# One encoder layer on one core: the last plain up-projection tiles become Strassen steps

## The chip, the core and the metric

The kernel runs on one core of a Trainium2 chip. The core has a matmul engine (TensorE, PE in the profile, with its weight loads as PEld), three engines for element-wise work (VectorE or DVE, ScalarE or ACT, GpSimd or POOL), a queue engine that starts transfers (SyncE or SP), 16 DMA engines that all queues share, an on-chip memory of 128 partitions (SBUF) and eight accumulation banks behind TensorE (PSUM). The engines run side by side and wait for each other by semaphores; each of ACT, DVE and POOL works through its own instructions strictly in order.

The metric is the device time of one execution in microseconds (us). Before the change the median of three runs is 526.61 us (526.12 to 527.57).

## The reference, cut to what matters

The layer is an RMSNorm, a combined input projection, a recurrent head group and an attention head group, an output projection, a residual sum, and an MLP. The change lies in the first half of the MLP:

```python
x = x + mix @ w_out[l]                                   # x: 512 rows of 1024
h = rms_norm(x, mlp_norm_g[l])
x = x + jnp.square(jax.nn.relu(h @ w_up[l])) @ w_down[l]   # w_up: 1024 x 4096
```

All of it is float32. The kernel leaves the normalising factor of `h` to the end (relu and square let it through as its square), so the up-projection multiplies the transposed rows of `x`, scaled by the gain, and the result is scaled per row when it is added to `x`.

## The kernel before, in words

**Precision.** TensorE takes a reduced float32 form, so each operand is split in two: a high part (a copy that rounds) and a low part (what the copy lost). `mm3` (L311) makes one product from three matmuls: high by high, high by low, low by high. Each weight chunk of 128 x 1024 is loaded to a raw tile, its high part `whi` is copied by ACT (`conv_hi`, L240) and its low part `wlo` is subtracted by DVE (`conv_lo`, L261). `feed` (L299) asks for both three chunks ahead of the chunk that TensorE multiplies.

**The MLP's halves.** The 4096 columns of `w_up` are done in two halves of 16 tiles of 128 columns. A half has an up-projection, whose results are relu'd, squared and kept on chip, and then a down-projection with `w_down`. The names that matter: `pu` are the PSUM tiles of the up-projection, `pd` those of the down-projection.

**Plain tiles and Strassen steps.** A plain tile (`up_tile`, L1558) multiplies one 128-column tile by all 512 rows: 8 blocks of the inner dimension, each three matmuls of 512 columns, 24 in all. Four such tiles can also be done as one group by one level of Strassen's scheme: inner dimension, columns and rows are cut in two, and seven products of sums take the place of eight. Each of the seven steps (`up_step`, L1574) has 24 matmuls of 256 columns. The kinds are named by their operands: `11`, `21` and `22` take a block of the weights as it is, `t1` to `t4` take sums of weight blocks (t1 = 12 + 11, t2 = t1 + 22, t3 = 12 + 22, t4 = t2 + 21). On the side of the rows, `11`, `21` and `t4` take unsummed quadrants, and `t1`, `t2`, `t3` and `22` take sums (`h_sums`, L1331), which DVE builds and which are then split into `hh` and `hl` (`split_h`, L1597). The sums are also written to DRAM (`hsd`) and read back for the second half.

**The results of a group.** The seven products collect in three PSUM banks (a, b, c). `quad_evac` (L1372) copies a bank aside on ACT after `11`, `t1` and `t2`, adds a copy and a bank on DVE after `22`, `t3` and `21`, and takes a relu on ACT after `t4`; the squares follow on ACT two steps later where `ON_ACT` (L58) says so, else on DVE. When two groups that belong together are done, DVE makes the sums for the down-projection (`up_pair`, L1285) and `next_a` begins to split them.

**The weight sums.** A raw tile `tw` takes block 12 by an ordinary load from SP, and blocks are added by transfers that accumulate, which only POOL's queue can start (`load_t`, L1177). t2 is made by such a transfer onto t1's tile once t1 is split (L277); t4 and t3 are made by DVE (L286, L281).

**Which group is what, and in which order.** `STEPS` (L54) is written out by hand for each half: before, the first half has four plain tiles (`n0` to `n3`) and three groups (4, 8, 12), the second half four groups (0, 8, 12, 4). Three plain tiles run side by side at the head of the first half (L1522 to L1531), the rows 4 to 7 of the transposed operand being turned by TensorE after their first block; the operand sums are made beside them. What is done beside a step is hung on it by hand in `late` (L1614): operand splits, the row squares `x1_sq` (L1267), loads. ACT, DVE, POOL and PE work in the order of the program; SP does not: its transfers are sent as soon as their buffers are free, in an order that a scheduler sets at build time.

**Ahead of the MLP.** The second half of the output projection is itself done by seven Strassen steps (`OSEQ`, L62); beside its last steps (`BES`, L1243) the first rows of the operand are turned (`h2_t`, L1207, and their low parts, `h2_l`, L1219) and the first weights are split.

**Buffers.** Raw weights: three stream tiles `wraw` and four `tw`. Split weights: four `whi` and four `wlo`. The four tiles `ts` that the down-projection will need share one large buffer with the residual rows `x1`, which are last read when the output projection ends. PSUM: four banks `pj`, two `gs`, two `et`.

Of the kernel before, what the change touches and what calls it, by code (L numbers as in the profile page):

```python
# [44 lines left out]
for _n, _w in (("w0", 4), ("w1", 4), ("w2", 4), ("w3", 4), ("cb", 4),  # L45
# [19 lines left out]
def up_steps(h):  # L65
    return [("n", int(s[1:])) if s[0] == "n" else (s.split(":")[1], int(s.split(":")[0])) for s in STEPS[h].split()]
# [32 lines left out]
def hybrid_kernel(ctx: ExitStack, tc, xw0, xw, xn, w_in, w_v, w_out, w_up, w_dn, gates, vecs, bias, fg, out):  # L99
# [90 lines left out]
    cu, cq, cd_ = {}, {}, []  # L190
    for h in range(2):
        for kind, f0 in up_steps(h):
            if kind == "n":
                cu[h, f0] = len(chunks)
                chunks.append(w_up[h * HF + f0])
            else:
                cq[h, f0, kind] = len(chunks)
                chunks.append((h, kind, f0, "u"))
# [37 lines left out]
    for (h, f0, kind), i in cq.items():  # L236
        if kind == "11" and (h, f0) != (0, 4):
            swap[i], swap[i + 1] = i + 1, i
# [22 lines left out]
    def conv_lo(i):  # L261
        if i < len(chunks):
# [11 lines left out]
            if isinstance(c, tuple) and len(c) == 4:  # L274
# [4 lines left out]
                elif kind == "22":  # L279
                    t = raws[cq[h, f0, "t3"]]  # L280
                    nc.vector.tensor_tensor(t, t, r, op=OP.add)  # L281
                elif kind in ("t2", "21"):
# [894 lines left out]
    def load_t(half, n, f0):  # L1177
        t = work.tile([P, 1024], FT, name="tw", tag="tw", bufs=4)
        nc.sync.dma_start(t, ublock(half, "12", f0))
        for b in {"t1": ("11",), "t2": ("11", "22"), "t3": ()}[n]:  # L1180
            nc.gpsimd.dma_start(t, ublock(half, b, f0), accum_op=OP.add)
        raws[cq[half, f0, n]] = t

# [65 lines left out]
    BES["s1"].update({1: lambda: (o_lo("22", 0), o_lo("22", 1), h2_t(0, "pj")), 2: lambda: h2_t(1, "pj"), 3: lambda: (conv_lo(C_WA + 8), h2_l(0))})  # L1249
    BES["22"].update({1: lambda: (h2_t(2, "pj"), h2_l(1)), 2: lambda: (h2_t(3, "pj"), conv_lo(C_WA + 9)), 3: lambda: (h2_l(2), h2_l(3))})  # L1250
    for w in OSEQ:
# [7 lines left out]
        if w in ("s3", "s4", "21"):  # L1259
            load_t(0, {"s3": "t1", "s4": "t2", "21": "t3"}[w], 4)  # L1260
# [20 lines left out]

    def h2k(k):
        return (h2h[:, k, :], h2l[k])
# [29 lines left out]
    def up_evac(ff, p):  # L1313
        q, c = ff // 2, slice((ff % 2) * TH, (ff % 2 + 1) * TH)
        for t in range(2):
            if (q, t) not in rb:
                rb[q, t] = g_("a")
            act(rb[q, t][:, c], p[:, t * TH:(t + 1) * TH], AF.Relu)
        if ff % 2:
            for t in range(2):  # L1320
                nc.vector.tensor_tensor(rb[q, t], rb[q, t], rb[q, t], op=OP.mult)
                rb_done.add((q, t))
            up_pair(q)


# [5 lines left out]
    def h_sums(k):  # L1331
        m, c = k // 2, slice((k % 2) * TH, (k % 2 + 1) * TH)
        if k % 2 == 0:
            for n in SUMS:
                hsum[n, m] = g_("hsum")
        a, b = hm.pop(k), hm.pop(k + 4)
        e, s2, s3, s4 = [hsum[n, m][:, c] for n in SUMS]
        nc.vector.tensor_tensor(e, b[:, right], a[:, right], op=OP.subtract)
        stt(s2, a[:, left], -1.0, e, op0=OP.mult, op1=OP.subtract)
        nc.vector.tensor_tensor(s3, a[:, left], a[:, right], op=OP.subtract)  # L1340
        stt(s4, b[:, left], -1.0, s2, op0=OP.mult, op1=OP.subtract)
# [156 lines left out]
    def load_s1(half, ts, qs=range(NQ)):  # L1498
        for q in qs:
            t = ts[:, q, :]  # L1500
            nc.sync.dma_start(t, wblock(half, "11", q))
            nc.gpsimd.dma_start(t, wblock(half, "12", q), accum_op=OP.add)
            raws[cd_[half] + 2 * q + 1] = t
# [9 lines left out]
    for half in range(2):  # L1513
        c0, cd = cu.get((half, 0)), cd_[half]
# [4 lines left out]
        start = 0  # L1519
        if half == 0:  # L1520
            start = 3
            pu = [ps_("pu", "pj") for _ in range(start)]  # L1522
            for k in range(KD):
                if k == 1:
                    for j in range(4, 8):
                        h2_t(j, "gs" if j < 6 else "et")
                        h2_l(j)
                for i in range(start):
                    mm3(pu[i], wk(c0 + i, k), h2k(k), k == 0, k == KD - 1)
                    if i == 0:  # L1530
                        feed(c0, k)  # L1531
                if k in (2, 3, 4, 5):
                    h_sums(k - 2)
                if k == 6:
                    x1_sq(0, 0)
                if k in (5, 7):
                    h_hi("t1", k // 7)
# [269 lines left out]
```

## Time and profile before

| | |
|---|---|
| median of three runs | 526.61 us (526.12 to 527.57) |
| the profiled execution | 526.41 us, its span 524.6 us |
| mean granted TensorE clock | 0.998 |
| busy in the span: PE, DVE, ACT, POOL | 517.3, 430.8, 350.1, 63.9 us |
| first up-projection | 201.1 to 285.2 us of the span |
| second up-projection | 361.4 to 442.0 us |

A row of the timeline holds the start and the duration of an instruction in us, its engine, its line, what it writes and reads by the program's names, and its shape. Matmuls overlap, so what one costs is the distance from its start to the next one's. A row of a line's answer has the number of instructions and their shortest, median and longest duration in ns. A row of the transfers ends with the size of each and the median time from its issue to its landing, in us. A row of windows has the stretch, its length, then the busy time and the count of PE, PEld, DVE, ACT and POOL, the clock, the share of the DMA engines and GB/s.

### The profile page before, as it was taken

The numbers are of one execution on the slowest core, as the hardware profiler recorded it, in microseconds if no ns is written. First come the engines' busy times: TensorE is split into PE (matmuls) and PEld (weight loads), VectorE is DVE, ScalarE is ACT, GpSimd is POOL, SyncE is SP. The second block draws the span as 40 slices with busy tenths as digits, with TensorE's granted clock in tenths as the row PEclk, the third lists the DMA queues.
The fourth block names the chain that finished last, engine by engine and source line by source line (L and its number), as shares of the span: only waits on it lengthen the run. The fifth ranks groups of instructions, "written<-read, shape, count | busy, mean of one in ns | idle before, by whom it ended". The sixth has DMA issues, their size and how long they took to land.

```text
span 524.6 us, 8196 instructions
## 1 busy us (share of the span) xinstructions
PE 517.3 (99%) x3021; PEld 442.9 (84%) x3021; DVE 430.8 (82%) x669; ACT 350.1 (67%) x566; POOL 63.9 (12%) x88
## 2 busy tenths in 40 slices
PE   9999999999999999999999999999999999999995
PEld 7857888777787688899999888889999999888884
DVE  6998985788887998898789987789656978986985
ACT  6579946668865748585578666565476677655664
POOL 0183000000000221001300312001101300131000
PEclk9999999999999999999999999999999999999999
DMA  7736545367696299848595899976978497799704
GB/s 287 226 89 198 161 150 180 102 171 212 186 295 207 62 188 277 323 130 196 131 229 135 222 272 280 305 269 161 300 221 202 113 229 214 157 286 264 183 1 161
DMA packets 39961, 104.62 MB, mean 199 GB/s; under 512 B 4944, under 2 KB 13264, under 8 KB 39920
## 3 DMA queue, kind: packets, MB, share of 16 engines
q1 hardware_dynamic: 32368, 78.10, 44.5%
q0 software_dynamic: 7408, 25.79, 26.7%
q8 instruction: 24, 0.39, 0.3%
q10 hardware_dynamic: 144, 0.20, 0.1%
q14 instruction: 17, 0.14, 0.1%
HBM read 95.59 MB, written 4.29 MB: 190 GB/s over the span
## 4 chain that ended last, share of the span: by engine, by line
PE 96%; DVE 2%; DMA 1%; SPq 0%; issue 0%; ACT 0%; DVEq 0%; ACTq 0%
PE pu L312 10%; PE pu L314 10%; PE pu L313 10%; PE pd L314 10%; PE pd L312 10%; PE pd L313 10%; PE pqk L312 3%; PE pqk L314 3%; PE pqk L313 3%; PE pwo L312 2%; PE pav L942 2%; PE pwo L314 2%; PE pwo L313 2%; PE pt L842 2%; PE ps L806 2%; PE pp L312 1%
## 5 line engine op out<-in xcount | busy, mean ns | idle before, releaser
L269 DVE TENSOR_TENSOR wlo<-wraw,whi 128x1024 fp32r<-128x1024 f32 x71 | 86.6, 1220 | 23.8 <-ACT whi L247 23.6
L247 ACT ACTIVATE whi<-wraw 128x1024 fp32r<-128x1024 f32 x67 | 70.7, 1056 | 32.4 <-PE pd L314 17.9
L313 PE MATMUL pd<-wlo,ah 128*128 128x512 f32 (+1 forms) x195 | 75.2, 386 | 0.0
L312 PE MATMUL pd<-whi,ah 128*128 128x512 f32 (+1 forms) x195 | 75.2, 386 | 0.0
L314 PE MATMUL pd<-whi,al 128*128 128x512 f32 (+1 forms) x195 | 75.2, 386 | 0.0
L247 ACT ACTIVATE whi<-tw 128x1024 fp32r<-128x1024 f32 x38 | 40.2, 1060 | 39.3 <-DMA tw<-in_w_up_dram 11.5
L313 PE MATMUL pu<-hl,whi 128*128 128x256 f32 x224 | 63.4, 283 | 0.0
L314 PE MATMUL pu<-hh,wlo 128*128 128x256 f32 x224 | 63.4, 283 | 0.0
L312 PE MATMUL pu<-hh,whi 128*128 128x256 f32 x224 | 63.4, 283 | 0.0
L269 DVE TENSOR_TENSOR wlo<-tw,whi 128x1024 fp32r<-128x1024 f32 x38 | 46.4, 1221 | 17.7 <-ACT whi L247 17.7
L312 PE MATMUL pu<-h2h,whi 128*128 128x256 f32 (+1 forms) x200 | 60.1, 300 | 0.0
L313 PE MATMUL pu<-h2l,whi 128*128 128x256 f32 (+1 forms) x200 | 60.0, 300 | 0.0
L314 PE MATMUL pu<-h2h,wlo 128*128 128x256 f32 (+1 forms) x200 | 60.0, 300 | 0.0
L312 PEld LDWEIGHTS pu<-hh,whi 128*128 128x128 f32 x224 | 43.0, 192 | 0.0
L313 PEld LDWEIGHTS pu<-hl,whi 128*128 128x128 f32 x224 | 43.0, 192 | 0.0
L314 PEld LDWEIGHTS pu<-hh,wlo 128*128 128x128 f32 x224 | 43.0, 192 | 0.0
L313 PEld LDWEIGHTS pd<-wlo,ah 128*128 128x128 f32 x195 | 36.6, 188 | 7.4
L314 PEld LDWEIGHTS pd<-whi,al 128*128 128x128 f32 x195 | 36.6, 188 | 7.3
L312 PEld LDWEIGHTS pd<-whi,ah 128*128 128x128 f32 x195 | 36.6, 188 | 7.3
L247 ACT ACTIVATE whi<-ts 128x1024 fp32r<-128x1024 f32 x24 | 25.4, 1060 | 25.7 <-PE pd L314 16.4
L313 PEld LDWEIGHTS pu<-h2l,whi 128*128 128x128 f32 x200 | 38.3, 191 | 1.3
L312 PEld LDWEIGHTS pu<-h2h,whi 128*128 128x128 f32 x200 | 38.3, 191 | 1.3
(275 smaller groups left out, 1214.8 us busy)
## 6 DMA issues: line engine op xcount, KB each, us to landing
wraw<-in_w_up_dram SPq DMA_DIRECT2D x25, 512.0 KB, 4.0
ts<-in_w_dn_dram POOLq DMA_DIRECT2D x24, 512.0 KB, 13.2
wraw<-in_w_dn_dram SPq DMA_DIRECT2D x24, 512.0 KB, 8.8
tw<-in_w_up_dram SPq DMA_DIRECT2D x15, 512.0 KB, 9.0
tw<-in_w_up_dram POOLq DMA_DIRECT2D x15, 512.0 KB, 8.0
wraw<-in_w_in_dram SPq DMA_DIRECT2D x13, 512.0 KB, 4.2
ts<-in_w_dn_dram SPq DMA_DIRECT2D x8, 512.0 KB, 6.5
tw<-in_w_dn_dram SPq DMA_DIRECT2D x8, 512.0 KB, 7.2
```

The source lines that it names most:

```text
L247: act(hi, raws[i], AF.Copy)
L269: nc.vector.tensor_tensor(lo, r, f(splits[i][0]), op=OP.subtract)
L312: nc.tensor.matmul(o, lhsT=a[0], rhs=b[0], start=bool(first), stop=False, skip_group_check=on)
L313: nc.tensor.matmul(o, lhsT=a[0], rhs=b[1], start=False, stop=False, skip_group_check=on)
L314: nc.tensor.matmul(o, lhsT=a[1], rhs=b[0], start=False, stop=bool(last), skip_group_check=on)
L806: nc.tensor.matmul(psq[p, u][e][:, :NK], lhsT=qs_[p, a][r, P * qt:P * qt + P], rhs=kks[p][r, b, w:w + NK], start=i == 0, stop=i == 2)
L842: nc.tensor.transpose(pt[:, i * P:(i + 1) * P], en[h][qt][:, k:k + P], ident)
L942: nc.tensor.matmul(pav[p][a, co], lhsT=vs[:, jt, h * DH:(h + 1) * DH], rhs=et[h, jt][:, ci], start=jt == 0 and i == 0, stop=jt == 3 and i ...
```

## The change

All 28 steps of the first half become Strassen steps, in a new order that begins with products of unsummed operands. In parts:

- `STEPS`, `QUADS`: the plain tiles go, group 0 comes; the first half is 0:11 8:11 4:11 0:21 8:21 0:t1 4:21 8:t1 and so on.
- Operand sums (`h_sum`): made one kind at a time, t1 and t2 on DVE, t3 and 22 on POOL, hung on the first steps. POOL has twelve instructions of 128 x 256.
- Weight sums of the first half: t4 of all four groups by an accumulating transfer (`RAW`), t3 of groups 0 and 8 too (`ADDED`); DVE keeps the t3 of 4 and 12.
- Squares of group 4 move from DVE to ACT, like those of the others (`ON_ACT`).
- The first step does its products with the operand's low parts last in each half (`head`).
- The rows 4 to 7 are turned inside the first two steps (`turn`); before, in one go after the first block. In the output projection's last steps the turns come one place earlier, and the low parts of two weight chunks move into the first step.
- The evacuations of the 21 blocks of groups 0, 8 and 4 are put off (`later`, `put`).
- Four of the eight row squares and the signs `nr2` move into the down-projection.
- The plain loads of `ts` and the accumulating transfers onto them are issued apart (`load_s1`, `add_s1`).

The diff, cut to its core:

```diff
-    "n0 n1 n2 4:11 4:t1 n3 4:t2 4:21 4:22 4:t3 8:11 8:t1 4:t4 8:t2 8:21 8:22 8:t3 12:11 12:t1 8:t4 12:t2 12:22 12:t3 12:21 12:t4",
+    "0:11 8:11 4:11 0:21 8:21 0:t1 4:21 8:t1 0:t2 0:22 0:t3 8:t2 4:t1 8:22 0:t4 8:t3 4:t2 8:t4 4:22 4:t3 12:11 12:t1 4:t4 12:t2 12:22 12:t3 12:21 12:t4",
...
-QUADS = ((4, 8, 12), (0, 8, 12, 4))
-ON_ACT = {(h, f, k) for h in range(2) for f in QUADS[h] if (h, f) != (0, 4) for k in ("21", "22", "t3", "t4")}
+QUADS = ((0, 8, 4, 12), (0, 8, 12, 4))
+AJ = {(0, 4), (1, 0)}
+ADDED = {(0, 0), (0, 8)}
+RAW = {(0, 0), (0, 4), (0, 8), (0, 12)}
+ON_ACT = {(h, f, k) for h in range(2) for f in QUADS[h] for k in ("21", "22", "t3", "t4")}
...
-                elif kind == "22":
+                elif kind == "22" and (h, f0) not in ADDED:
                     t = raws[cq[h, f0, "t3"]]
                     nc.vector.tensor_tensor(t, t, r, op=OP.add)
+                elif (h, f0) in RAW and kind == "t2":
+                    nc.gpsimd.dma_start(r, ublock(h, "21", f0), accum_op=OP.add)
+                    raws[cq[h, f0, "t4"]] = r
+                elif (h, f0) in RAW and kind == "21":
+                    emit_dma()
...
-    BES["s1"].update({1: lambda: (o_lo("22", 0), o_lo("22", 1), h2_t(0, "pj")), 2: lambda: h2_t(1, "pj"), 3: lambda: (conv_lo(C_WA + 8), h2_l(0))})
-    BES["22"].update({1: lambda: (h2_t(2, "pj"), h2_l(1)), 2: lambda: (h2_t(3, "pj"), conv_lo(C_WA + 9)), 3: lambda: (h2_l(2), h2_l(3))})
+    BES["s1"].update({1: lambda: (o_lo("22", 0), o_lo("22", 1), h2_t(0, "pj")), 2: lambda: h2_t(1, "pj"), 3: lambda: (h2_t(2, "pj"), h2_l(0))})
+    BES["22"].update({0: lambda: h2_l(1), 1: lambda: (h2_t(3, "pj"), h2_l(2)), 2: lambda: (h2_l(3), conv_hi(C_WA + 9)), 3: lambda: None})
...
-        if w in ("s3", "s4", "21"):
-            load_t(0, {"s3": "t1", "s4": "t2", "21": "t3"}[w], 4)
+        if w in ("s3", "s4", "21", "s1"):
+            load_t(0, *{"s3": ("t3", 0), "s4": ("t1", 0), "21": ("t1", 8), "s1": ("t1", 4)}[w])
...
+        if n == "t1":
+            nc.vector.tensor_tensor(o, b[:, right], a[:, right], op=OP.subtract)
+        elif n == "t2":
+            stt(o, a[:, left], -1.0, hsr["t1", m][:, c], op0=OP.mult, op1=OP.subtract)
+        elif n == "t3":
+            nc.gpsimd.tensor_tensor(o, a[:, left], a[:, right], op=OP.subtract)
+        else:
+            nc.gpsimd.tensor_tensor(o, a[:, left], b[:, left], op=OP.subtract)
+            nc.gpsimd.tensor_tensor(o, o, hsr["t1", m][:, c], op=OP.add)
         if k % 2:
-            for i, n in enumerate(SUMS):
-                nc.sync.dma_start(hsd[i][:, m * S:(m + 1) * S], hsum[n, m])
+            nc.sync.dma_start(hsd[SUMS.index(n)][:, m * S:(m + 1) * S], hsr[n, m])
...
+            head = half == 0 and (kind, f0) == ("11", 0)
...
+                if head:
+                    nc.tensor.matmul(o, lhsT=w[0], rhs=x[0], start=first, stop=False, skip_group_check=True)
+                    nc.tensor.matmul(o, lhsT=w[1], rhs=x[0], start=False, stop=False, skip_group_check=True)
+                    for k in range(4) if n % 4 == 3 else ():
+                        sl = slice((4 * e + k) * P, (4 * e + k + 1) * P)
+                        nc.tensor.matmul(o, lhsT=hi[:, sl], rhs=h_part(kind, k)[1], start=False, stop=n == 7 and k == 3, skip_group_check=True)
+                else:
+                    mm3(o, w, x, first, n == 7, True)
...
-                if n == 6:
+                if n == 6 and (half, kind, f0) != (0, "t2", 12):
                     next_a()
-            quad_evac(kind, f0, bank, keep, (half, f0, kind) in ON_ACT)
+            if half == 0 and kind == "21" and f0 < 12:
+                later.append(lambda: quad_evac("21", f0, bank, keep, True))
+            else:
+                quad_evac(kind, f0, bank, keep, (half, f0, kind) in ON_ACT)
...
+            late.update({(0, "11", 0): lambda: conv_lo(C_WA + 8), (0, "11", 3): lambda: conv_lo(C_WA + 9), (0, "11", 6): turn((4, 5)), (8, "11", 1): turn((6, 7)),
+                         (0, "11", 1): sums(*[("t3", k) for k in range(4)]), (8, "11", 0): sums(("t1", 0), ("t1", 1)), (8, "11", 5): split_h("t1", 0),
+                         (4, "11", 0): sums(("t1", 2), ("t1", 3), ("22", 0), ("22", 1), ("22", 2), ("22", 3)),
+                         (4, "11", 1): split_h("t1", 1), (0, "21", 0): sums(("t2", 0), ("t2", 1)),
+                         (0, "21", 5): split_h("t2", 0), (8, "21", 0): sums(("t2", 2), ("t2", 3)), (8, "21", 5): split_h("t2", 1),
+                         (0, "t1", 5): split_h("22", 0), (4, "21", 5): split_h("22", 1),
+                         (0, "t3", 3): put, (8, "t2", 3): put, (0, "t4", 3): put, (8, "t1", 1): split_h("t3", 0), (0, "t2", 1): split_h("t3", 1),
+                         (8, "t1", 5): lambda: load_t(0, "t3", 8, False), (0, "22", 1): lambda: add_t(0, "t3", 8),
+                         (8, "t2", 5): lambda: load_t(0, "t3", 4), (0, "t4", 5): lambda: load_t(0, "t1", 12, False), (4, "t2", 2): lambda: add_t(0, "t1", 12),
+                         (4, "t3", 5): lambda: load_t(0, "t3", 12),
+                         (0, "22", 7): xt(0, 0), (8, "t2", 7): xt(0, 1), (8, "22", 7): xt(1, 0), (4, "t2", 5): xt(1, 1), (4, "22", 5): room,
...
+            if half == 0 and j < 4:
+                x1_sq(2 + j // 2, j % 2)
```

More of the change, by code (lines that the diff above doesn't have):

```diff
@@ L236, in hybrid_kernel @@
     for (h, f0, kind), i in cq.items():
-        if kind == "11" and (h, f0) != (0, 4):
+        if kind == "11" and h:
             swap[i], swap[i + 1] = i + 1, i
@@ L1513, in hybrid_kernel @@
     for half in range(2):
-        c0, cd = cu.get((half, 0)), cd_[half]
+        cd = cd_[half]
         rb_done.clear()
@@ L1518, in hybrid_kernel, with room @@
         todo = deque((w, q) for _, w, q in seq)
[L1519 to L1537, printed above, removed]
[L1538 to L1546 removed]
+        def room():
             nonlocal ts
             ts = big.tile([P, NQ, 1024], FT, name="ts", tag="bigA")
[L1549 to L1551 removed]
         def next_a():
@@ L1615, in hybrid_kernel @@
         qs = QUADS[half]
-        for f0, f1 in zip(qs, qs[1:]):
+        for f0, f1 in zip(qs, qs[1:]) if half else ():
             late[f0, "t2", 0] = lambda f1=f1: load_t(half, "t1", f1)
@@ L1626, in hybrid_kernel @@
         if half == 0:
-            late[8, "t3", 4], late[12, "11", 4], late[12, "t2", 1], late[12, "t2", 7] = [load_1(q) for q in range(4)]
+            late[4, "t3", 4], late[12, "11", 4], late[12, "t2", 1], late[12, "t2", 7] = [load_1(q) for q in range(4)]
         else:
             late[12, "t3", 4], late[4, "11", 4], late[4, "t2", 1], late[4, "t2", 7] = [load_1(q) for q in range(4)]
-        for kind, f0 in up_steps(half)[start:]:
+        for kind, f0 in up_steps(half):
             ready = set(opdone)
             st["step"] = st.get("step", 0) + 1
-            if kind == "n":
-                up_tile(f0, late)
-            else:
-                up_step(kind, f0, late)
+            up_step(kind, f0, late)
         while pend_sq:
@@ L1700, in hybrid_kernel @@
                 load_s3(half, q)
+            if half == 0 and j < 4:
+                x1_sq(2 + j // 2, j % 2)
+                nr2[j] = consts.tile([P, 1], FT, name="nr2_%d" % j)
+            if half == 0 and j == 4:
+                for tt in range(4):
+                    nc.vector.tensor_scalar(nr2[tt], r2[tt], -1.0, None, op0=OP.mult)
             if half == 0 and j == 16:
```

114 lines of the change are left out of this document (40 added, 74 removed).

## The prediction

> **What bounds the kernel now.** I read the page first, then what TensorE waits for, then the stages by windows, then single rows of the timeline.
>
> ```profile
> span 524.6 us, 8196 instructions
> PE 517.3 (99%) x3021; PEld 442.9 (84%) x3021; DVE 430.8 (82%) x669; ACT 350.1 (67%) x566; POOL 63.9 (12%) x88
> ...
> PE 96%; DVE 2%; DMA 1%; SPq 0%; issue 0%; ACT 0%; DVEq 0%; ACTq 0%
> ```
> ```profile
> PE pwarm L142 <- PEq L1796: 0.8, 1, 0.8
> PE pxr L453 <- ACT h_hi L353: 0.2, 1, 0.2
> ```
> ```profile
> 201.10:219.25 18.15, 18.15 (x90) 15.17 (x89) 14.37 (x29) 9.69 (x18) 0.00 (x0) 1.00 1.02 349
> 201.10:285.10 84.00, 84.00 (x617) 80.06 (x616) 71.41 (x108) 56.48 (x92) 6.92 (x8) 1.00 0.72 204
> 285.10:345.00 59.90, 59.90 (x266) 49.63 (x266) 49.78 (x62) 36.87 (x49) 10.36 (x12) 1.00 1.01 270
> 361.30:442.00 80.70, 80.70 (x674) 80.66 (x674) 61.11 (x66) 52.77 (x73) 8.63 (x10) 1.00 0.77 207
> ```
>
> TensorE is 96% of the chain, and the only waits recorded for it are 1.0 us at the start. The window rows (length, then busy PE, PEld, DVE, ACT, POOL, clock, DMA share, GB/s) show it full in the first up-projection (201.1 to 285.1) and in the second (361.3 to 442.0). So a matmul taken out here is worth its spacing, as long as ACT, DVE and the transfers keep delivering; nothing else in this stage shortens the kernel.
>
> **The term that is removed.** The spacing comes from starts:
>
> ```profile
> 201.09 0.40 PE L312 MATMUL pu<-h2h,whi 128*128 128x512 f32 x1
> ...
> 203.15 1.95 PE L1214 MATMUL pxt<-ident,x1n 128*128 128x128 f32 x16
> 204.85 0.48 PE L312 MATMUL pu<-h2h,whi 128*128 128x512 f32 x1
> ...
> 285.18 0.40 PE L312 MATMUL pd<-whi,ah 128*128 128x512 f32 x1
> ...
> 361.37 0.28 PE L312 MATMUL pu<-h2h,whi 128*128 128x256 f32 x1
> ...
> 442.00 0.40 PE L312 MATMUL pd<-whi,ah 128*128 128x512 f32 x1
> ```
>
> The first up-projection lasts 285.18 - 201.09 = 84.09 us: four plain tiles (96 matmuls of 512 columns), 21 Strassen steps and 16 transposes, which take 204.85 - 203.15 = 1.70. The second is already what the first becomes, 28 steps of 24 matmuls of 256 columns: 442.00 - 361.37 = 80.63, or 2.88 a step. With the same 16 transposes the first would last 82.33, and some 0.1 more because they now come in two groups with a slow matmul after each (0.48 in the 204.85 row). **Gain if nothing is late: 84.09 - 82.4 = 1.7 us.** The chain has no other idle time here to win, so this is also the most the change can bring.
>
> **What the other engines get.** Durations:
>
> ```profile
> L1377 ACT ACTIVATE v<-pu x9: 597/598/635, 223.4 to 273.9; 128x512 f32<-128x512 f32 x9
> L1395 ACT ACTIVATE a<-a x5: 614/615/621, 260.4 to 283.3; 128x512 f32<-128x512 f32 x5
> L1396 ACT ACTIVATE a<-a x5: 632/632/634, 261.0 to 284.0; 128x512 f32<-128x512 f32 x5
> L1318 ACT ACTIVATE a<-pu x8: 367/386/413, 218.9 to 230.9; 128x256 f32<-128x256 f32 x8
> L247 ACT ACTIVATE whi<-wraw 128x1024 fp32r<-128x1024 f32 x67 | 70.7, 1056 | 32.4 <-PE pd L314 17.9
> L269 DVE TENSOR_TENSOR wlo<-wraw,whi 128x1024 fp32r<-128x1024 f32 x71 | 86.6, 1220 | 23.8 <-ACT whi L247 23.6
> L281 DVE TENSOR_TENSOR tw<-tw,wraw x3: 1216/1218/1221, 230.6 to 267.9; 128x1024 f32<-128x1024 f32 x3
> L1338 DVE TENSOR_TENSOR hsum<-hm x4: 417/418/419, 209.2 to 214.7; 128x256 f32<-128x256 f32 x4
> L1387 DVE TENSOR_TENSOR a<-v,pu x9: 669/678/689, 236.7 to 283.4; 128x512 f32<-128x512 f32 x9
> ```
>
> ACT: three more weight copies (3 x 1.06), three copies out of PSUM and a relu for quad 0 (4 x 0.60), squares of quads 0 and 4 (six pairs of 0.62 + 0.63, two single ones at the same 0.62), less eight 256-wide relus (8 x 0.39) and four row squares of the same size that move into the down-projection (4 x 0.62): 3.2 + 2.4 + 8.7 - 3.1 - 2.5 = +8.7, so 56.5 becomes 65 of 82.4 us (79%). The moved squares lie beside TensorE there: ACT has 36.87 busy of 59.90; without that cover they would cost 2.5. DVE: three more low parts (+3.7) and three PSUM sums (+2.0), less four of the six weight sums (-4.9), eight 256-wide operand sums (-3.4), four squares of plain tiles and four of quad 4 (8 x 0.69, -5.5): -8.1, to 63 of 82.4. On average both have room, ACT less than anywhere now. What is late is decided in two narrow places, so I follow the chains.
>
> **The head, where I expect the gain to go.** Before, the plain tiles gave DVE 18 us to build the operand sums. Now the steps begin: 0:11 at 201.1 and, with 8 transposes inside each of the first two steps, step 2 at 208.7, step 4 (8:21) at 214.4, step 5 (0:t1, the first that needs a sum) at 217.3, step 8 (0:t2) at 225.9.
>
> ```profile
> 203.21 1.78 SPq L1501 DMA_DIRECT2D ts<-in_w_dn_dram  x4
> ...
> wraw<-in_w_up_dram SPq DMA_DIRECT2D x25, 512.0 KB, 4.0
> ...
> ts<-in_w_dn_dram SPq DMA_DIRECT2D x4, 512.0 KB, 8.0
> ...
> 202.44 0.74 DVE L1204 SCALAR_TENSOR_TENSOR x1n<-pwo,nrc,x 128x512 f32<-128x512 f32 x1
> ...
> 203.82 0.69 ACT L1215 ACTIVATE h2h<-pxt,vt 128x512 fp32r<-128x512 f32 x1 [1.94 <-PE pxt L1214]
> ...
> 207.83 0.74 ACT L1217 ACTIVATE hm<-pxt,vt 128x512 f32<-128x512 f32 x1
> ```
>
> SP issues the four loads of `ts` as soon as the last `x1n` (202.44 + 0.74) frees their buffer, long before their place in the program, and they take 8.0 us to land. Block 8:21 needs the stream buffer of 8:11, whose low part now stands behind that `x1n` on DVE: it is requested right after the four, and I put its landing at 212. ACT is in order: it has the copies of the transposed rows (0.57 apart, eight from about 203.9, with one PSUM copy between) until 209, then stands at `whi` of 8:21 until 212. From there: `whi` 213, its low part on DVE 214.3 (step 4 just served), `hl` of t1 (0.6) 214.9, two sums t1 (0.7) 215.6, `hh` 216.2, `whi` of 0:t1 217.2, `wlo` 218.4. Step 5 wanted it at 217.3: **1.1 us late**.
>
> Edits of the head that I take at nothing: the low parts of 8:11 and 4:11 (1.1 apart on DVE, done by 205) are used at 204.9 and 208.7, the second with cover, the first with 0.7 between its end at 203.6 + 0.6 for a sum of GpSimd and its use; the two groups of transposes lie where the one lay, 2 us into the stage, behind the same `x1n`. The first step takes the high parts of all four rows in its first 1.0 us, where the plain tiles took one row in 0.7 us and the next two later; their transposes are one slot earlier, so I bound this by 0 and one low part (0.69, as a sum of the same width in the L1387 row) and take 0. The late evacuations of the 21 blocks only hold PSUM banks that step 26 is the next to need.
>
> GpSimd now also works there. The trace has no operation of 128x256 on it; the nearest rows:
>
> ```profile
> 1.00 0.29 POOL masks.py:199 TENSOR_SCALAR_AFFINE_SELECT ident<-ident 128x128 f32<-128x128 f32 x1
> ...
> 29.94 0.20 POOL L163 TENSOR_TENSOR pl<-pl,z 128x8 f32<-128x8 f32 x1
> ...
> 31.99 0.67 POOL L163 TENSOR_TENSOR pl<-pl,z 128x8 f32<-128x8 f32 x1
> ...
> 29.09 1.28 DVE L496 TENSOR_TENSOR xr<-pxr,rrow 128x512 f32<-128x512 f32 x2
> ...
> 31.85 0.75 DVE L505 SCALAR_TENSOR_TENSOR xc<-xr,vt,xc 128x511 f32<-128x511 f32 x1
> ```
>
> The same 128x8 product takes 0.20 beside a DVE instruction with one operand in PSUM and 0.67 beside one with two in SBUF: the two exclude each other there. A 256-wide sum is bounded below by DVE's own 0.42 and above by 0.1 + 4 x 0.19 = 0.86 (twice the columns and twice the operands of the select's 0.29, less 0.1 fixed); I take 0.6, near the middle. Of the twelve, nine run while DVE stands idle or behind other waits; the last three wait for the t1 sums at 215.6 and fall between DVE's own instructions. One of them ahead of the low part of 0:t1 adds 0.6. (The accumulate for t2 stands behind them on GpSimd's queue, which is free by 217.5, before it is wanted.) **Late in all: 1.7 us**, just the gain. (The Trainium skill, "SBUF — State Buffer", section "Who interferes with whom", states that a VectorE instruction with two SBUF inputs and a GpSimd one that reads SBUF lock each other out for the whole instruction; the rows agree. Its "GPSIMD Engine Reference", "Elementwise — side-by-side cycle accounting", has about 2.6 cycles an element at 1.2 GHz; by that a 256-wide sum would be an estimated 0.55, and the lateness 1.65.)
>
> **The accumulating transfers.** Half 0 goes from 7 to 14 of them on weights.
>
> ```profile
> q1 hardware_dynamic: 32368, 78.10, 44.5%
> q0 software_dynamic: 7408, 25.79, 26.7%
> ...
> tw<-in_w_up_dram POOLq DMA_DIRECT2D x1, 512.0 KB, 5.4
> ...
> tw<-in_w_up_dram POOLq DMA_DIRECT2D x1, 512.0 KB, 8.0
> ...
> tw<-in_w_up_dram POOLq DMA_DIRECT2D x2, 512.0 KB, 11.4
> ```
>
> By the queue rows one accumulate of 0.52 MB holds the 16 engines for 0.267 x 524.6 / 25.79 x 0.524 = 2.85 us, a plain load for 1.6. Seven more are 20 us on a stage with 0.72 x 84 = 60 in use, so nearly full. It lands in 5.4 alone, 8.0 beside a load, 11.4 beside another accumulate. Block t2 of quad 0 starts at 218.9 when 0:t1 is split, lands at 224.3 to 226.9, and is split 2.4 later: 226.7 to 229.3, against step 8 at 225.9 + 1.7 = 227.6, so nothing to 1.7 more. Then 0:t4, 8:t4, 8:t3 and 4:t2 are summed by transfers issued within some 10 us; ACT stands at 8:t3 until it lands, and all that is queued behind it (squares, PSUM copies, the next `whi`) with it. The copies run three steps, 8.6 us, ahead, and 2.4 of that is their own work, so up to 6 us of such waiting costs nothing; beyond that it does. I take nothing here and leave 0 to 2 in the range. The remaining four (t1 and t2, t4 of quad 12, t3) keep the distances of before within a step.
>
> **Forecast: no change.** -1.7 + 1.7 = 0. The profiled execution took 526.41 (span 524.6 and 1.8 around it), 0.2 under the median of 526.61; on the median, 526.6.
>
> **Rivals.**
> *Nothing is late.* If SP asks for 8:21 ahead of `ts`, it lands near 209 (the median load of this kind lands in 4.0), 0:t1 is split by 215.5 and even the GpSimd sums fit: 526.6 - 1.7 = 524.9. For it: DVE is relieved by 8 us; the second half runs the same 28 steps without a wait. Against: there the sums are read back ready-made, and in the first 18 us here the transfers are at 1.02 of their share.
> *GpSimd's sums hold DVE.* Place: from 215 to 219, between the t1 sums and the low part of 0:t1. Price: three sums of 0.42 to 0.86 in front instead of one, 1.3 to 2.6, so 0:t1 is 2.4 to 3.7 late, and the accumulate for t2 starts that much later: split at 227.5 to 231.3 against 225.9, up to 5.4 late. Net -1.7 + 2.4 to -1.7 + 5.4: 527.3 to 530.3, about 529. It is slower at all from 1.7 us of lateness, by more than 0.3% from 3.3. For it: the 0.67 beside the 0.20. Against: DVE's queue has an idle stretch before 213 that takes the other nine.
> *It doesn't do what it says*, the 256-wide pace not holding in the reordered first step, has no support: the pace of 0.12 is the same in every step shown.
>
> **How the numbers follow.** Forecast (partly or wholly paid back, 525.1 to 528.2): 0.46. Nothing late: 0.24. Held by GpSimd or by the accumulates behind it: 0.30. The bound of 0.3% (1.6 us), about what a measurement of this kernel can tell from no change, lies at 525.0 and 528.2: faster 0.22 (most of the first rival), same 0.47, slower 0.31. The range holds the whole gain with the scatter of the runs below it and most of the slower rival: 524.6 to 530.0.
>
> **What would show it.** Right: the window from the first `pu` to the first `pd` near 84 us with 82.4 of matmuls; a wait of `pu` for `wlo` about 16 us into the stage; `whi` on ACT waiting for a DMA of `wraw` before it; GpSimd sums near 0.6 each. Wrong: no wait of `pu` at all (524.9); the wait at a later step, behind a `tw` transfer, would say that the accumulates and not the head decide; GpSimd sums over 0.9 or DVE instructions stretched beside them would say the slower rival.

## The result, and the profile after

The change made the kernel slower: 535.40 us (534.04 to 536.88) against 526.61 us, a ratio of 1.0172 with an interval of 1.0161 to 1.0184. The profiled execution took 535.4 us.

From the page of the changed kernel, first the span and the busy times, then the chain of work that ended last; and from its waits, those of PE (releaser, total, times, longest):

```profile
span 533.6 us, 8371 instructions
...
PE 520.7 (98%) x3093; PEld 448.8 (84%) x3093; DVE 428.5 (80%) x655; ACT 360.0 (67%) x579; POOL 82.0 (15%) x107
...
PE 84%; DMA 6%; DVE 5%; ACT 3%; issue 1%; POOL 0%; DVEq 0%; ACTq 0%; POOLq 0%
```

```profile
PE pu L316 <- DVE a L1382: 4.3, 1, 4.3
PE pu L318 <- DVE wlo L268: 1.3, 2, 0.8
```

Nearly all that was added lies in one stage. Of the 9.0 us by which the span grew, 8.1 lie between the first `pu` and the first `pd`: the first up-projection now takes 201.89 to 294.10, 92.21 us, where it took 84.09. What follows is 239.4 us before and 239.5 now, and 0.8 us lie ahead of the stage. Its start differs by up to 1.5 us among the profiled executions of kernels with the same code ahead of it (200.56 in e12, 202.09 in e1), so below each kernel is judged by this stage as well as by its time.

The stage by stretches, as windows (PE, PEld, DVE, ACT and POOL busy with their counts; granted clock; DMA share; GB/s): first the kernel before, then the changed one.

```profile
217.00:235.00 18.00, 18.00 (x121) 16.65 (x120) 16.15 (x22) 15.56 (x31) 0.00 (x0) 1.00 0.51 177
235.00:251.00 16.00, 16.00 (x136) 16.00 (x135) 13.57 (x23) 8.98 (x17) 1.71 (x2) 1.00 0.75 180
```

```profile
201.89:294.10 92.21, 86.47 (x689) 85.16 (x688) 69.46 (x86) 64.25 (x98) 21.84 (x24) 0.96 0.82 215
217.00:235.00 18.00, 16.74 (x136) 16.21 (x135) 13.89 (x18) 11.91 (x18) 3.65 (x4) 1.00 0.95 249
235.00:251.00 16.00, 15.88 (x133) 15.67 (x132) 7.79 (x12) 8.78 (x15) 2.58 (x3) 1.00 0.96 241
259.90:265.40 5.50, 5.49 (x26) 5.50 (x27) 2.93 (x5) 4.12 (x8) 0.00 (x0) 0.50 0.61 203
```

Two things are to be seen. From 217 to 251 the DMA engines are at 0.95 of their share, where they were at 0.51 and 0.75; the mean over the stage, 0.82, hides it. And from 259.9 to 265.4 PE is busy all the time but does only 26 matmuls: the granted clock is 0.50 there.

PE itself, around its long wait (its timeline; matmuls follow each other at 0.12):

```profile
255.34 0.28 PE L318 MATMUL pu<-hh,wlo 128*128 128x256 f32 x1
259.91 0.55 PE L316 MATMUL pu<-h2h,whi 128*128 128x256 f32 x1 [4.30 <-DVE a L1382]
```

That is step 17, 8:t4: 4.57 from start to start, 4.45 more than the pitch. How it came about stands in the chain of waits of that stretch, read from its end upwards (start, duration, what):

```profile
219.45 7.12 DMA tw<-in_w_up_dram
...
232.14 1.15 DVE wlo L268
233.31 6.31 DMA tw<-in_w_up_dram
239.66 0.47 issue
240.15 0.53 POOL tw L1190
240.68 9.65 DMA tw<-in_w_up_dram
250.35 1.06 ACT whi L246
...
255.83 0.95 ACT whi L246
256.84 1.11 issue
257.95 1.22 DVE tw L280
259.16 0.61 DVE a L1382
```

The low part of 0:t3 (done 233.3) frees a `tw` buffer; only then is the block for t3 of group 8 loaded (6.31). When it has landed GpSimd can issue the accumulate onto it (L1190, 240.15) and, behind that on its queue, the one for t2 of group 4 (240.68), which takes 9.65. ACT stands for both:

```profile
247.21 1.06 ACT L246 ACTIVATE whi<-tw 128x1024 fp32r<-128x1024 f32 x1 [5.99 <-DMA tw<-in_w_up_dram]
...
250.35 1.06 ACT L246 ACTIVATE whi<-tw 128x1024 fp32r<-128x1024 f32 x1 [0.41 <-DMA tw<-in_w_up_dram]
...
255.73 1.05 ACT L246 ACTIVATE whi<-wraw 128x1024 fp32r<-128x1024 f32 x1
```

Between 247 and 257 ACT hardly pauses: squares, PSUM copies and high parts have queued up behind the wait. On DVE the evacuation of 8:t3 (`a`, L1382) stands in order behind the low part of 4:22, which waits for ACT's 255.73, and behind the sum for t3 of 4:

```profile
256.80 1.23 DVE L268 TENSOR_TENSOR wlo<-wraw,whi 128x1024 fp32r<-128x1024 f32 x1 [1.39 <-ACT whi L246]
257.95 1.22 DVE L280 TENSOR_TENSOR tw<-tw,wraw 128x1024 f32<-128x1024 f32 x1
259.08 0.68 DVE L1382 TENSOR_TENSOR a<-v,pu 128x512 f32<-128x512 f32 x1
```

PE has finished 8:t3 at 255.6 and needs that bank for 8:t4: it waits until 259.77.

In all the stage loses 0.31, 0.66, 0.92, 0.29, 0.16 and 4.45 us of waiting (at 203, 218, 228, 249, 252 and 255) and 2.3 us by the clock (25 matmuls at 0.213 in place of 0.12): 9.1, on the 82.4 that its matmuls and transposes need at their pitch: 91.5 of the 92.2 measured.

### The profile page after: what moved, and what is told of

It reads as the page before. It is cut to its first block, busy times and chain, and to the rows that moved or that the text cites. A ratio compares the mean times of both kernels' runs of the same rounds, so it can differ in the third digit from the quotient of the medians.

```text
span 533.6 us, 8371 instructions
## 1 busy us (share of the span) xinstructions
PE 520.7 (98%) x3093; PEld 448.8 (84%) x3093; DVE 428.5 (80%) x655; ACT 360.0 (67%) x579; POOL 82.0 (15%) x107
## 4 chain that ended last, share of the span: by engine, by line
PE 84%; DMA 6%; DVE 5%; ACT 3%; issue 1%; POOL 0%; DVEq 0%; ACTq 0%; POOLq 0%
PE pd L318 9%; PE pd L317 9%; PE pd L316 9%; PE pu L316 7%; PE pu L318 7%; PE pu L317 7%; DMA tw<-in_w_up_dram 4%; PE pqk L316 3%; PE pqk L318 3%; PE pqk L317 3%; PE pav L946 2%; PE pt L846 2%; PE ps L810 2%; PE pwo L316 2%; DMA wraw<-in_w_up_dram 1%; PE pwo L318 1%
## 5 line engine op out<-in xcount | busy, mean ns | idle before, releaser
L246 ACT ACTIVATE whi<-wraw 128x1024 fp32r<-128x1024 f32 x66 | 69.5, 1055 | 31.8 <-PE pd L318 16.6
L318 PE MATMUL pu<-hh,wlo 128*128 128x256 f32 x256 | 72.8, 285 | 1.4 <-DVE wlo L268 1.3
L316 PE MATMUL pu<-hh,whi 128*128 128x256 f32 x256 | 72.7, 284 | 0.0
L317 PE MATMUL pu<-hl,whi 128*128 128x256 f32 x256 | 72.5, 283 | 0.0
L316 PE MATMUL pu<-h2h,whi 128*128 128x256 f32 x184 | 53.3, 290 | 4.3 <-DVE a L1382 4.3
L318 PE MATMUL pu<-h2h,wlo 128*128 128x256 f32 x184 | 53.1, 289 | 0.0
L317 PE MATMUL pu<-h2l,whi 128*128 128x256 f32 x184 | 53.1, 289 | 0.0
L318 PEld LDWEIGHTS pu<-hh,wlo 128*128 128x128 f32 x256 | 49.1, 192 | 2.2 <-DVE wlo L268 2.2
L316 PEld LDWEIGHTS pu<-hh,whi 128*128 128x128 f32 x256 | 49.2, 192 | 0.1
L317 PEld LDWEIGHTS pu<-hl,whi 128*128 128x128 f32 x256 | 49.2, 192 | 0.0
L268 DVE TENSOR_TENSOR wlo<-ts,whi 128x1024 fp32r<-128x1024 f32 x24 | 29.3, 1222 | 12.2 <-ACT whi L246 12.1
```

The lines of the kernel that those rows point to most:

```text
L246: act(hi, raws[i], AF.Copy)
L268: nc.vector.tensor_tensor(lo, r, f(splits[i][0]), op=OP.subtract)
L316: nc.tensor.matmul(o, lhsT=a[0], rhs=b[0], start=bool(first), stop=False, skip_group_check=on)
L317: nc.tensor.matmul(o, lhsT=a[0], rhs=b[1], start=False, stop=False, skip_group_check=on)
L318: nc.tensor.matmul(o, lhsT=a[1], rhs=b[0], start=False, stop=bool(last), skip_group_check=on)
```

## The experiments

Three theories at the start. **A**: one late block, that of 8:t3 (loaded late, then accumulated late), makes ACT stand and, in order behind it, the evacuation on DVE. **B**, a rival of the prediction: GpSimd's operand sums hold DVE. **C**: there are too many accumulating transfers. Every time below stands beside runs of the kernel before on the same chip (medians of 526.1 to 526.6 us). "Stage" is from the first `pu` to the first `pd` in the one profiled execution, which can lie off the median (that of e6 is its slowest, 535.67, that of e7 its fastest, 526.64).

| | median us | ratio to before, interval | stage us |
|---|---|---|---|
| before | 526.61 | | 84.09 |
| changed | 535.40 | 1.0172 [1.0161, 1.0184] | 92.21 |
| e1 t3 of 8 on DVE | 527.44 | 1.0029 [1.0018, 1.0040] | 85.26 |
| e2 evacuation first | 532.82 | 1.0132 [1.0116, 1.0149] | 89.54 |
| e3 sums on DVE | 536.05 | 1.0191 [1.0176, 1.0206] | 93.27 |
| e4 two accumulates fewer | 533.48 | 1.0142 [1.0121, 1.0162] | 90.33 |
| e5 fifth buffer | 533.84 | 1.0147 [1.0132, 1.0163] | 90.22 |
| e6 head order | 533.88 | 1.0148 [1.0133, 1.0163] | 92.69 |
| e7 = e1 + e6 | 527.38 | 1.0016 [1.0007, 1.0025] | 84.78 |
| e8 = e7, t3 of 0 on DVE | 527.46 | 1.0019 [1.0010, 1.0028] | 84.63 |
| e9 = e4 + e5 | 527.60 | 1.0023 [1.0014, 1.0032] | 84.85 |
| e10 = e7, `ts` late, split earlier | 525.55 | 0.9991 [0.9977, 1.0005] | 82.73 |
| e11 = e5, `ts` late | 533.68 | 1.0142 [1.0128, 1.0156] | 90.18 |
| e12 = e10 without `ts` late | 526.94 | 1.0013 [1.0004, 1.0022] | 84.69 |
| e13 = e5, accumulate ahead | 532.07 | 1.0100 [1.0083, 1.0117] | 89.90 |
| e14 = e13 + head of e10 | 530.22 | 1.0075 [1.0063, 1.0088] | 85.49 |
| e15 = e10, sums on DVE | 524.81 | 0.9968 [0.9956, 0.9980] | 82.36 |

### The late block, the evacuation and the sums (e1 to e3)

e1 takes the one transfer away:

```diff
-ADDED = {(0, 0), (0, 8)}
+ADDED = {(0, 0)}
```

> One name changed: the sum t3 of group 8 is made by DVE again (ADDED holds group 0 alone), so one accumulating transfer goes. Theory A (the late t3 block): ACT stands 6.0 us at the high part of 8:t3, everything in order behind it is late, the evacuation of 8:t3 on DVE among it, TensorE waits 4.45 us at step 17 and then runs 25 matmuls at half clock (2.3 us more). It expects ACT's long wait gone, no wait of step 17, no halved clock: 535.4 - 6.8 = 528.6 us, 528 to 530. Theory B (the recorded one: GpSimd's sums hold DVE in the head): unchanged, 535 to 536. Theory C (too many accumulating transfers in all): the wait moves to the next one, 4:t2, and stays over 3 us: 531 to 535.

527.44: 8 us of the loss gone, the long wait and the half clock with it, as A has it. Waits of 0.30, 0.66, 0.83 and 0.86 us at 203, 218, 228 and 234 are left.

e2 lets DVE evacuate 8:t3 before it turns to the low part of 4:22:

```diff
-                feed(c, n)
+                if not (half == 0 and (kind, f0, n) == ("t3", 8, 4)):
+                    feed(c, n)
...
+            if half == 0 and (kind, f0) == ("t3", 8):
+                conv_lo(c + 3)
```

> Order on DVE alone: in step 15 the low part of 4:22 comes behind the evacuation of 8:t3 instead of ahead of it; all transfers stay. Theory A with its last link (an evacuation queued behind a low part that waits for ACT): ACT's 6.0 us at 8:t3 stays as it is, TensorE's wait at step 17 falls under 1 us and the clock stays whole: 528.5 to 530.5 us. If the lateness of the weights itself is what costs (theory C), TensorE waits for a low part one step on instead, over 2 us: 532 to 536. Theory B: 535 to 536.

532.82, more than A said and in C's range, though PE does not wait over 2 us for one low part as C had it. The waits of PE in e2:

```profile
PE pu L316 <- ACT v L1372: 2.4, 3, 1.4
PE pu L318 <- DVE wlo L268: 1.4, 3, 0.8
PE pu L316 <- DVE a L1382: 0.8, 2, 0.5
```

The long wait is cut up, not removed: 0.70, 0.67, 0.43, 0.65 and 1.53 us at five steps between 254 and 282, 3.98 for the 4.45. ACT's lateness is passed on to whatever comes next. What e2 did remove is the half clock (1.00 granted from 256 to 268 us), and its stage is 2.67 us shorter than the changed kernel's, about the 2.3 put down to it. So my expectation took the order on DVE for the cause; it only decides whether the lateness falls in one piece.

e3 puts GpSimd's twelve sums on DVE (the three `nc.gpsimd.tensor_tensor` of `h_sum` become `nc.vector.tensor_tensor`).

> The twelve operand sums t3 and 22 run on DVE in the same places and with the same two-operation form; GpSimd makes none. Theory B: the 2 us that TensorE loses in the first nine steps go and with them the later wait: 528 us or less. Theory A: DVE gets 12 x 0.34 = 4.1 us more in the head, GpSimd no longer holds it; the waits of the head change by at most 1 us either way and the wait at step 17 stays: 534 to 537.

536.05, as A said, and the wait at 8:t4 stays with 3.46 us: B isn't the cause of the loss. In the head A was wrong: its waits should have changed by at most 1 us, and grew from 1.9 to 4.0. Of that, 0:t2 alone waits 2.06, for an accumulate that landed 9.2 us after its issue.

### What keeps the block late (e4, e5, e9, e11, e13)

e4 leaves out the accumulates of block 21 into t4 of groups 0 and 8 (so t4 lacks block 21 there):

```diff
-                    nc.gpsimd.dma_start(r, ublock(h, "21", f0), accum_op=OP.add)
+                    if f0 not in (0, 8):
+                        nc.gpsimd.dma_start(r, ublock(h, "21", f0), accum_op=OP.add)
```

> Leaves out the block 21 in the sums t4 of groups 0 and 8 (their two accumulating transfers are not sent; t4 is then t2). The t3 block of group 8 still has its load after the buffer is free and its accumulate after the load. If other transfers in flight make it late (theory C, or A with congestion), the load takes about 4 and the accumulate 5.4 to 6, it lands near 243 instead of 247.2, ACT waits 2 us or less, step 17 is served: 528 to 530. If the two transfers in a row are the cause by themselves, ACT still waits 4 us or more and TensorE over 2: 532 to 535. Theory B: 535.

533.48, as for two transfers in a row, and the wait stays at 4.0. The two remaining accumulates go out at 237.74 and 238.28 and land at 243.6 and 249.0. The transfers of e4 in two windows, 238.3 to 243.6 and 243.6 to 249.0 (queue, packets, MB, share of 16 engines):

```profile
q0 software_dynamic: 144, 0.52, 62.2%
q1 hardware_dynamic: 89, 0.36, 20.5%
```

```profile
q1 hardware_dynamic: 293, 1.07, 52.9%
q0 software_dynamic: 144, 0.52, 50.2%
```

Each window holds one block of 0.52 MB on the accumulating queue, in 5.3 and in 5.4 us, though the plain loads beside it went from 0.36 to 1.07 MB. **Two accumulates issued 0.5 us apart were served one after the other, at over 5 us each.** So the second lands some 11 us after its issue.

e5 gives the load of that block a buffer of its own (`tag="tw", bufs=5` in place of 4, `NG = 43` in place of 45).

> A fifth tw buffer (paid for with two of the 45 general ones), so that the load of the t3 block of group 8 no longer waits for the low part of 0:t3 (233.3 us in the changed kernel) and its accumulate goes out some 5 us earlier. If that late start is the cause of the 4.45-us wait: most of the wait and the half clock behind it go, 529 to 531.5 us. If there are simply too many accumulating transfers in these 40 us, they are as many as before: 533 to 536 us.

533.84, only 1.6 us better. The load was early now, but the accumulate went out only at 235.66, behind that of 8:t4 on GpSimd's queue, which waited until 235.08 for a low part; three blocks in a row landed the last of them at 248.4. e9 joins both edits.

> e4 and e5 together: five tw buffers and the accumulates of block 21 into t4 left out for groups 0 and 8 (so t4 lacks block 21 there). Alone each moved the time by 2 us or less. If the late block needs both, an early start and transfers that are not crowded, the wait for it goes: 527 to 529.5 us. If two accumulating transfers in a row on one queue are by themselves too slow (5 us or more each): a wait of 1.5 to 3 us at 8:t4 stays, 530 to 533 us.

527.60, the wait gone: alone the two are worth 1.9 and 1.6 us, together 7.8. e11 asks whether the 2 MB of `ts` loads at 210 and 223 are what crowds the queue in e5, and issues them late on GpSimd's queue:

```diff
-        nc.sync.dma_start(ts[:, q, :], wblock(half, "11", q))
+        (nc.sync if half else nc.gpsimd).dma_start(ts[:, q, :], wblock(half, "11", q))
```

> As e5 (five tw buffers, all accumulates kept), with the four loads of ts issued late by GpSimd. If the 2 MB of ts loads in the stretch are what crowds the transfers: 528.5 to 531.5 us. If the accumulates crowd one another: 532.5 to 534.5 us.

533.68: they aren't. e13 keeps every transfer and only moves that accumulate ahead of 8:t4's:

```diff
-(0, "22", 1): lambda: add_t(0, "t3", 8)
+(8, "t1", 6): lambda: add_t(0, "t3", 8)
```

> As e5 (fifth tw buffer, all accumulates kept), with the accumulate into t3 of group 8 put one place earlier on GpSimd's queue, ahead of that of 8:t4, which waits until 235.1 us for a low part. If its place behind that waiting accumulate is what kept the block late in e5: ACT finds the block in place, no long wait of PE, 527 to 529 us. If the accumulates crowd one another whatever their order: ACT still stands 3 us or more for a tw block, 531 to 534.5 us.

532.07: between the two. Block 8:t3 is now in place in time (ACT doesn't wait for it), but the next one is not. GpSimd's issues in e13, then ACT's next wait for a `tw`:

```profile
222.95 0.85 POOL L276 DMA_DIRECT2D tw<-in_w_up_dram  x1 [3.34 <-DVE wlo L268]
228.31 0.85 POOL L282 DMA_DIRECT2D tw<-in_w_up_dram  x1 [4.51 <-DVE wlo L268]
228.89 1.15 POOL L1190 DMA_DIRECT2D tw<-in_w_up_dram  x1
235.68 0.85 POOL L282 DMA_DIRECT2D tw<-in_w_up_dram  x1 [5.65 <-DVE wlo L268]
237.12 0.85 POOL L276 DMA_DIRECT2D tw<-in_w_up_dram  x1 [0.58 <-DVE wlo L268]
```

```profile
248.27 1.06 ACT L246 ACTIVATE whi<-tw 128x1024 fp32r<-128x1024 f32 x1 [4.06 <-DMA tw<-in_w_up_dram]
```

With the one issued at 218.74, six blocks pass until 248.3, 4.9 us each; ACT wanted the last at 244.2. With one block fewer (e1) the same block, issued at 237.87, lands at 245.3, and ACT waits 0.38 us for it. So A was right in naming the block and incomplete on why, and C is right in a sharper form: beside the plain loads of this stretch the queue passes a block in about 5 us, and six of them (t2 of 0, t2 of 8, t4 of 0, t3 of 8, t4 of 8, t2 of 4) don't fit between 218.7, when the first can start, and 244.

### The head (e6 to e8, e10, e12, e14, e15)

e6 moves only the splits of the t1 sums, so that 0:t1 is split ahead of them:

```diff
-(8, "11", 5): split_h("t1", 0)
+(4, "11", 5): split_h("t1", 0)
...
-(4, "11", 1): split_h("t1", 1)
+(0, "21", 1): split_h("t1", 1)
```

> Only the two splits of the t1 sums are moved, from 8:11 and 4:11 to 4:11 and 0:21, so that the split of block 0:t1 goes ahead of them and the accumulate of t2 of group 0 starts 2 us earlier; the accumulate into t3 of group 8 stays. If the head and the late block are two separate losses: 533 to 534.5 us, the waits at 218 and 228 us smaller by about 1.5 us in all and the wait at 8:t4 still 3 to 5 us. If the lateness of the head is what makes the late block late: under 530 us.

533.88, stage 92.69: within what A said, but not by its way; the waits of the head changed place (0.58 at 218, 1.63 at 234) and didn't shrink.

> t3 of group 8 summed on DVE, and the splits of the t1 sums moved as in e6: both losses repaired. With the two waits for low parts (0.66 and 0.83 us) gone from 527.4: 525.5 to 526.3 us, about even with the kernel before or slightly better. If the head's waits are not set by the order on DVE and ACT but by GpSimd's sums: 527 to 527.8 us.

527.38, a miss of 1 us, and in the range that was given for GpSimd's sums. The trace shows another cause: PE waits 1.07 at 233 for a PSUM copy on ACT, which stands behind a high part that waited for the accumulate into t2 of 8 (issued 222.26, landed 231.9). The same mechanism once more, at an earlier block.

> As e7, and t3 of group 0 is summed on DVE too, so that all three weight sums are off the transfers. If only the transfer into group 8's block matters: within 0.4 us of e7. If the number of accumulating transfers matters by itself: 0.5 us or more below e7. If DVE is short of time here (one more instruction of 1.22 us near 230 us): 0.5 to 1.2 us above e7.

527.46: no difference, so the accumulate into t3 of group 0, which is issued before the stage, does no harm.

e10 splits the second t1 sum at `(4, "11", 6)` and takes the `ts` edit of e11; e12 is e10 without that edit.

> As e7 (t3 of group 8 on DVE), with the split of the second t1 sum one place earlier than in e7 and the four loads of ts issued by GpSimd at their place in the program (near 255 us and later) instead of by SP at 210 and 223 us. If those loads slow the accumulates into t2 of groups 0 and 8: both waits of PE near 232 and 218 us shrink, the stage comes to 83.0 to 84.2 us and the time to 525.3 to 526.6 us. If the accumulates are slow of themselves: 526.8 to 527.5 us.

> e10 with the loads of ts back on SP, so that against e7 only the split of the second t1 sum is one place earlier. If that order made the difference between e7 (stage 84.78 us) and e10 (82.73 us): 525.2 to 525.9 us, no wait at 218 nor at 233 us. If the 2 MB of ts loads crowd the accumulate into t2 of group 8: the wait near 233 us stays, 526.4 to 527.2 us.

e10 came to 525.55, stage 82.73, with one wait of 0.30 left; e12 to 526.94, stage 84.69. The `ts` loads are worth 2.0 us of stage here, 1.4 by the medians, and were worth nothing in e11, where the later wait took up whatever was saved. e14 puts the same repairs beside the kept transfers:

> e13 with the other repairs of e10 (splits of the t1 sums later, ts loads late by GpSimd), so that all three weight sums stay transfers. If e13 removes the wait: about e10, 525.2 to 526.4 us. If crowding remains: 527 us or more, with a wait of PE for a block that comes by an accumulate.

530.22: the head is clean, and a wait of 2.60 us for the evacuation at 8:t4 remains, by the sixth block again (issued at 233.99, landed at 245.3). (The runs lie 3.8 above the kernel before: 1.4 of it is in the stage, and in the profiled execution `pd` waits another 1.7 for ACT behind it.)

> e10 with the twelve operand sums of GpSimd on DVE again. In e3 this cost nothing and gained nothing, but the large wait lay over it. If GpSimd's sums lengthen DVE's own instructions by as much as they would take on DVE: the stage within 0.3 us of e10's 82.73, 525.2 to 525.9 us. If they do take work off DVE: its sums ahead of the first low parts make the head late, 0.6 to 1.5 us above e10. If they hold DVE up: no more than e10, with DVE less busy in the stage.

524.81, 0.9968 [0.9956, 0.9980]: faster than the changed kernel, and by 0.3% than the kernel before. The stage as a window, in e10 and in e15:

```profile
200.62:283.35 82.73, 82.69 (x690) 82.46 (x688) 70.18 (x86) 63.93 (x98) 22.20 (x25) 1.00 0.81 220
```

```profile
201.42:283.78 82.36, 82.36 (x689) 82.35 (x688) 70.38 (x98) 64.22 (x98) 12.47 (x16) 1.00 0.84 223
```

PE has no wait at all in e15's stage; e10's 0.30 at 202 us is gone. DVE has twelve instructions more and is busy 0.2 us longer: the sums on GpSimd had taken nothing off it. That is the first of the three cases, with a gain somewhat larger than its range (0.37 us of stage in place of 0.3 at most). By the medians it is 0.7; the rest is not in this stage, and e10's profiled execution has one more wait of 0.6 us in the second up-projection.

## Why the prediction was wrong

The forecast was 526.6, a gain of 1.7 us paid back by 1.7 us of lateness. The gain is there, but the stage loses 9.1 us, 6.8 by waits and 2.3 by the clock.

1. **The gain was right.** 84.09 - 82.4 = 1.7 us, if nothing is late: e15's stage is 82.36, and its time is 1.6 us under the kernel before.

2. **The engines.** ACT was put at 65 us and has 64; DVE at 63 and has 69.5. The sums moved to GpSimd were counted as taken off DVE, and came back as longer DVE instructions: e15 puts twelve of 0.42, 5.0 us, back on DVE, and it is busy only 0.2 us longer. The rest of the 6.5 isn't traced.

3. **The head: right in size by luck.** Predicted 1.7 us late, measured 0.31 + 0.66 + 0.92 = 1.9 up to step 8, by another way: `ts` did not go ahead of 8:21 on SP (205.2 for the weights, 210.2 for the first two of `ts`). The low part of 0:t1, beside a GpSimd sum, began at 217.39 and took 1.76 in place of 1.22, and cost 0.66 and not 1.7; the accumulate into t2 of 0 landed 7.1 after its issue and cost 0.92, inside the "nothing to 1.7 more" that I left out of the sum. The reordered first step, bounded by 0 and 0.69 and taken at 0, cost 0.31; e3 and e15, without GpSimd's sums, don't have that wait.

4. **The step that failed** is the one on the accumulating transfers: "up to 6 us of such waiting costs nothing; beyond that it does. I take nothing here". ACT did wait, 5.99 us at the very block named and 0.41 at 4:t2 behind it, and it cost 4.45 at 8:t4 and 0.45 just before. The slack was not 6 but about 1.5. Waits of ACT for 8:t3 and 4:t2 together, and the wait of PE at 8:t4 that followed:

| | ACT waits | PE waits |
|---|---|---|
| changed | 6.40 | 4.30 |
| e3 | 4.94 | 3.46 |
| e4 | 5.48 | 4.00 |
| e5 | 4.92 | 3.45 |
| e6 | 6.17 | 4.30 |
| e11 | 5.85 | 4.30 |
| e13 | 4.06 | 2.74 |
| e14 | 3.92 | 2.60 |

The difference is 1.3 to 2.1 in all eight, and in e10 a wait of 1.18 us of ACT for 4:t2 made none of PE. (e2, which has another order on DVE, is left out.) I had counted how far the weight copies run ahead of their own use, three steps less 2.4; but the same ACT and DVE also evacuate PSUM, and an evacuation is due when its step ends. The first thing late was not the block that came late, it was an evacuation queued behind its successors.

5. **Two inputs of that step were wrong too.** I had landing times of single transfers, 5.4 to 11.4 us, and did not add them up along the queue; in line, six took 29.5 us in e13 and 27.7 in e14, so that the sixth was late though 8:t3 no longer was. And the room was taken from the stage's mean ("nearly full", 80 of 84), when the six stand in 25 us of it. That the load of 8:t3 waits for the low part of 0:t3, because the four `tw` are taken, I didn't see at all: by the program its accumulate belongs to step 9, near 229, and it went out at 240.

6. **The half clock** was in no sum: 2.3 us.

7. Of the rivals, *GpSimd's sums hold DVE* shows its signs (sums of 0.73 to 1.72 us, where I took 0.6 and at most 0.86, a bound whose 0.1 of fixed cost stands in no row; DVE stretched). But its price, once the rest is repaired, is 0.37 us of stage, or 0.7 by the medians of e10 and e15, not 2.4 to 5.4; in e3, with nothing else repaired, taking the sums off GpSimd made the stage 1.1 us longer. *Nothing is late* is e15, after four repairs. The sign that was to speak for the accumulates, a wait at a later step behind a `tw` transfer, is what the trace shows.

## What to carry to other kernels

When a wait is put on an in-order engine, list everything that engine does for others and take the slack of the most urgent one; here that was a PSUM evacuation with 1.5 us, not the weight block with 6. When sums are moved from an engine to transfers, count them in the stretch where they stand and as a line on their queue, not one by one and not over the stage. And look for what was saved only after the largest later wait is gone: the `ts` loads were worth nothing in e11 and 2 us of stage in e10.

## What the runs showed of the hardware

- Accumulating transfers of 512 KB pass at 4.4 to 5.4 us each beside plain loads: 5.3 and 5.4 in e4's two windows, 4.9 for six in e13, and 4.4, by the bytes moved, in the changed kernel from 229.0 to 250.4, where this queue moved 2.54 MB in 63.1% of the engines' time and the plain loads 2.75 MB in 35.8%: 1.9 times the engine time for a byte.
- GpSimd's 128x256 sums took 0.73 to 1.72 us in the changed kernel, where DVE takes 0.42 for the same, and DVE's 128x1024 subtraction 1.76 beside them, where it takes 1.22. Twelve sums moved off DVE changed its busy time in the stage by 0.2 us.
- Waits of PE can halve its clock, for a time that comes in equal pieces. The window from 256 to 268 us, of the changed kernel, then of e13, then of e14; last, a window of e3's head:

```profile
256.00:268.00 12.00, 8.09 (x47) 8.12 (x48) 6.91 (x9) 9.24 (x15) 0.00 (x0) 0.72 0.71 199
```

```profile
256.00:268.00 12.00, 10.17 (x72) 10.20 (x73) 8.53 (x12) 9.04 (x14) 0.85 (x1) 0.86 0.54 135
```

```profile
256.00:268.00 12.00, 12.00 (x102) 12.00 (x101) 8.36 (x13) 7.72 (x13) 1.41 (x2) 1.00 0.55 162
```

```profile
229.09:234.50 5.41, 4.65 (x24) 4.45 (x25) 5.29 (x6) 5.41 (x9) 0.85 (x1) 0.69 0.58 90
```

  In windows of 1 us the clock of the changed kernel is 1.00 or 0.50, but for the two at the ends of the slow time. At either 1.0 or 0.5, the mean of 0.72 is 6.7 us of half clock, 0.86 is 3.4, and e3's 0.69 over 5.41 us is 3.4. Waits of 2.60 (e14) gave none, of 2.74, 3.45, 3.46 and 4.00 (e13, e5, e3, e4) one piece, of 4.30 one (e11) or two (the changed kernel, e6). But the piece in e3's head came after waits of only 1.90 and 0.76 us, 0.5 us apart, so the length of one wait does not decide it. The Trainium skill, "TensorE: Matmul & The Clock Gate", Part 1, has two states of the clock gate, half and full, and the half one after an idle window of about 3.4 us that runs freely: the pieces agree. That 2.74 us, or 1.90 and 0.76, were enough does not follow from a whole idle window, and why they were is left open.
